# A hybrid decoder layer on one core: a third k pair by seven products in V, two in the attention's output, and another order of the sums

## The chip, the cores and the metric

The kernel runs on one core of a Trainium2 chip. The metric is the device time of one execution in microseconds (us), lower is better. Before the change three runs took 1879.17, 1879.82 and 1880.22 us; the median is 1879.82. One further execution was taken by the hardware profiler; all profile rows are of it. The engines in the rows are PE (TensorE, matmuls), PEld (its weight loads), DVE (VectorE), ACT (ScalarE), POOL (GpSimd) and SP (SyncE, which issues the DMAs here).

## The reference

One layer on a residual stream of 256 tokens x 2048 channels, in float32. Weights and activations are float32, and the output too.

```
h = rmsnorm(x, g_mix);  proj = h @ w_in                # 2048 -> 2816+2816+5*2048
x_r, g_r, q, k, v, gate_r, gate_a = split(proj)
y_r = gelu(g_r) * rg_lru(causal_conv(x_r), ...)        # recurrent mixer
y_r = y_r @ w_rnn_out                                  # 2816 -> 2048
o   = stick_breaking_attention(norm(q), norm(k), v)    # 16 heads of 128
y_a = o @ w_attn_out                                   # 2048 -> 2048
x   = x + (sigmoid(gate_r) * y_r + sigmoid(gate_a) * y_a) @ w_o
g, u = split(rmsnorm(x, g_ffn) @ w_ffn_gu)             # 2048 -> 2 * 5632
x   = x + (silu(g) * u) @ w_ffn_down
x   = x + sigmoid(rmsnorm(x, g_ple) @ w_ple_gate) * (p @ w_ple_proj)
```

## The kernel before

**Precision.** TensorE multiplies a reduced float32 (fp32r). Each float32 operand is held as two such halves, hi (a rounded copy) and lo (the rest). A product of two operands is three matmuls into one PSUM bank, hi x hi, hi x lo and lo x hi (`prod`, L576 to L578), each 128x128 by 128x512.

**Weights.** All weights lie in one array in the order of use, cut into chunks of 128x1024 (512 KB). `Stream` brings them in: SP issues each chunk's DMA into one of 4 raw buffers (tile name `w`), ACT makes the high half (`whi`, L307) and DVE the low half (`wlo`, L308), each with 4 buffers. Splits run 3 chunks ahead of the matmuls and DMAs 4 more ahead. SP issues all DMAs in one order, each after its buffer came free. Activations, and raw weight blocks that are needed for sums, live in a pool of 26 tiles of 128x1024 (`Q`) and one of 21 tiles of 128x512 (`H`).

**Groups.** Wide products (`group`) make 256 tokens x 1024 columns at a time: two column halves of 512 and two token halves of 128, so four PSUM banks (the kernel names them 2, 4, 3, 8). A group works through a list of slots. A plain slot is one k tile of 128 input channels: 1 chunk and 12 matmuls. A pair of k tiles together with the two token halves and the two column halves is a 2x2 by 2x2 block product, which can be made by seven products in place of eight: 21 matmuls in place of 24. It needs sums of the weight blocks (made by DVE on the raw blocks, then split like a chunk) and sums of the activations (`half_sums`, called through `parts_sums`: an add of hi and lo, four 128x128 ops, an ACT copy, a DVE subtract), and four results that are shared: the products "11", T1, T2 and T3 are copied out of PSUM by ACT, and `whole` adds them to the four banks with four DVE ops.

**The lists.** `SEVEN` has two pairs of k tiles and 12 plain ones. A string names a slot for both pairs: "11", "21" and "22" are raw blocks (128x1024, one half for each pair), T1 starts as the raw block "12"; the rest are sums made in place by DVE (L291): T1 = 12 + 11, then T2, T3 and T4. `SEVEN3` has a third pair, whose seven products come in the slots ("S", 1, 2) to ("S", 4, 2): S1 and S2 are two raw chunks; for S2 DVE makes Y, a new `Q` tile, with two 512-wide adds (L266), S3 is S2 summed in place by one add, and S4 a half of Y with one more add. `LONG` is the list with two pairs of the recurrent output (ro). `pairs_of` names the pairs that a stage makes by seven products.

**The stages,** in the order in which PE runs them: a first gate block (gtr), the recurrent branch, the recurrent output (ro0, ro1), V (v0, v1), the blocks of Q, K and the attention's gate with the attention of eight pairs of heads worked in between (`step`, by the table `at`), the attention's output (ao0, ao1), w_o (wo0, wo1), gate-up groups gu0 to gu3, down (dn0), gu4 to gu7, down (dn1), gu8 to gu10, down (dn2), and the last gate (pg). A group number stands behind the stage's name.

**Around V.** The activation sums of V's pairs are made during the second recurrent output group (`also`, two of its slots). After each V group `whole` gives four result blocks, and each of them becomes one `Q` tile: ACT writes a scaled high half and DVE (L384) the low half.

**Around the attention's output.** `ost` holds the attention's output as eight `Q` tiles of hi and lo. Before, the two groups use a plain list, and each bank is multiplied by its gate (`gta`) and added to the gated recurrent output. `next_mix`, put in `pend` and taken by the next group's slots from the fourth on, turns a pair of these results by PE (L1041) for w_o.

**Order.** Each engine runs its instructions in the order of its own program. Where DVE's and ACT's instructions stand among each other was fixed when the kernel was built, by a scheduler with a model of their times; a tile that is asked for later in the code takes its place in the pool later.

Of the kernel before, what the change touches and what calls it, by code (L numbers as in the profile page):

```python
# [11 lines left out]
ALU = mybir.AluOpType  # L12

P = 128
S = 256
# [9 lines left out]
KD = D // P  # L25
# [5 lines left out]
FQ0 = [0, 16, 32]  # L31
NG = 11
SEVEN = ["11", "T1", "21", 4, 5, "22", 6, 7, "T2", 8, 9, "T3", 10, 11, "T4", 12, 13, 14, 15]
SEVEN3 = ["11", ("S", 1, 2), "T1", "21", ("S", 2, 2), 6, "T2", 7, "22", 8, ("S", 3, 2), 9, "T3", 10,
          ("S", 4, 2), 11, "T4", 12, 13, 14, 15]
def ONE(k):

    return [("S", 1), ("S", 2), k + 2, k + 3, k + 4, ("S", 3), k + 5, k + 6, ("S", 4), *range(k + 7, k + 12)]


LONG = ["11", "T1", "21", 4, 5, "22", 6, 7, 8, "T2", 9, 10, 11, "T3", 12, 13, 14, "T4", 15, 16, 17, 18, 19, 20, 21]
# [6 lines left out]
def pairs_of(name):  # L48

    if name[:2] == "dn":  # L50
        q = int(name[2])
        return [FQ0[q] // 2 + i for i in range(2 if FQ[q] == 16 else 1)]
    return (0, 1, 2) if name == "gu" else (0, 1)


def is_sum(x):

    return isinstance(x, str) or isinstance(x, tuple) and x[0] == "S"
# [14 lines left out]
C_XR, C_GR, C_Q, C_K, C_V, C_GTR, C_GTA = 0, 22, 44, 60, 76, 92, 108  # L73
# [87 lines left out]
def tail():  # L161


    def wide(name, w, slots, c=0):
        return [(name, g, w, c + 8 * g, c + 8 * g + 4, slots[g]) for g in range(2)]

    def blocks(*cs):
        return [("blk", b, None, c, None, None) for c, b in cs]

    def gu(*gs):  # L170
        return [("gu", g, "gu", 4 * g, 44 + 4 * g, SEVEN3) for g in gs]

    def dn(q):
        k, p = FQ0[q], FQ0[q] // 2
        slots = [x if isinstance(x, str) else x + k for x in SEVEN] if FQ[q] == 16 else [
            x if isinstance(x, int) else x + (p,) for x in ONE(k)]
        return wide(f"dn{q}", "dn", [slots] * 2)

    x = [("x", 0), ("x", 1)]
    plain = [list(range(KD))] * 2  # L180
    return (wide("ro", "ro", [LONG] * 2) + wide("v", "in", [SEVEN] * 2, C_V)
            + blocks(*[(c, b) for b in range(4) for c in (C_Q, C_K)], *[(C_GTA, b) for b in range(4)])
            + wide("ao", "ao", plain) + wide("wo", "wo", [SEVEN] * 2) + gu(0, 1, 2, 3) + dn(0) + gu(4, 5, 6, 7) + dn(1)
            + gu(8, 9, 10) + dn(2)
            + wide("pg", "pg", [SEVEN[:-3] + x + SEVEN[-3:]] * 2))

# [167 lines left out]
def tile_hybrid_block(ctx: ExitStack, tc: tile.TileContext, xT: bass.AP, x: bass.AP, pT: bass.AP,  # L354
# [18 lines left out]
    def psum():  # L373
        cnt[0] += 1
        return pps.tile([P, 512], F32, tag="ps", name=f"ps_{cnt[0]}")
# [4 lines left out]
    def tt(o, a, b, op):  # L380
        nc.vector.tensor_tensor(o, a, b, op)  # L381
# [4 lines left out]
    def actv(o, i, f, **kw):  # L386
        nc.scalar.activation(o, i, f, **kw)  # L387
# [234 lines left out]
    xg = []  # L622
# [20 lines left out]
    def group(at, pairs, sums, after=None, also=()):  # L643

        name, g = at  # L650
        slots = [x for n, y, _, _, _, sl in HEAD + TAIL if (n, y) == at for x in sl
                 if isinstance(x, int) or is_sum(x)]
        seq = [(n, q) for n, x in enumerate(slots) for q in products(x, pairs_of(name)[:2])]
        if at == LAST_GROUP:
            k = len(slots) - 3
            rest = [q for q in seq if q[0] >= k]
            seq = [q for q in seq if q[0] < k] + [q for b in "2438" for q in rest if q[1][0] == b]
        first, last = {}, {}
        for i, (_, (b, y, _, _)) in enumerate(seq):
            first.setdefault(b, i)  # L660
            last[b] = i
            if y in ("11", "T1", "T2", "T3"):
                last[y] = i
        plain8 = [i for i, (_, (b, y, _, _)) in enumerate(seq) if b == "8" and not isinstance(y, str)]
        assert "11" not in last or last["T1"] < plain8[0]
        banks, tile_, got = {}, {}, {}
        for i, (n, (b, y, p, c)) in enumerate(seq):
            if n not in got:
                if n in also:
                    also[n]()  # L670
                if n >= 3 and pend:
                    pend.pop(0)()
                got[n] = S_.take(("tok", name, g, slots[n]))
            if b not in banks:
                banks[b] = psum()
            ps = banks[b]
            if p is None:
                o = tok(pairs, *y)
            else:
                o = {"11": tok(pairs, 2 * p, 0), "21": tok(pairs, 2 * p + 1, 0), "22": sums[p][3],  # L680
                     "T1": sums[p][0], "T2": sums[p][1], "T3": sums[p][2],
                     "T4": tok(pairs, 2 * p + 1, 1)}[y]
            _, _, hi, lo, w0 = got[n].columns(c)
            s = slice(w0, w0 + 512)
            prod(ps, o, hi[:, s], lo[:, s], i == first[b], i in (last[b], last.get(y)),
                 b in "B8")
            if y in ("11", "T1", "T2", "T3") and i == last[y]:
                t = tile_[y] = tl("T")
                actv(t, ps, AF.Copy)
                if y == "T2":  # L690
                    tt(tile_["T1"], tile_["T1"], t, ALU.subtract)
                if y == "T3" and after is not None:
                    after(tile_)
        return [banks[b] for b in "2438"], tile_


    xc, xcs, gel, y, gtr, ysum, xsum = {}, {}, {}, [], [], {}, {}
# [120 lines left out]
    also = {max(1, 2 * i - 4): [later(next_xg)] for i in range(2, NPD)}  # L818
    for i in range(NPD):
        also.setdefault(2 * i + 1 if i < 7 else 14, []).append(squares_x(i))  # L820
    also = {n: (lambda fs: lambda: [f() for f in fs])(fs) for n, fs in also.items()}
# [38 lines left out]
    def whole(at, pairs, sums, also=()):  # L860

        (q2, q4, q3, q8), t = group(at, pairs, sums, None, also)
        c11, c21, c12, c22 = t["11"], t["T2"], t["T1"], t["T3"]
        tt(c11, q2, c11, ALU.add)
        tt(c21, q4, c22, ALU.add)
        tt(c12, q3, c12, ALU.add)
        tt(c22, q8, c22, ALU.subtract)
        return c11, c21, c12, c22

    def parts_sums(pairs, sums, p):  # L870
        h = tl("T")
        hi, lo = parts(pairs[p])
        tt(pair(h), f32(hi), f32(lo), ALU.add)
        sums[p] = half_sums(h)
# [8 lines left out]

    n = len(LONG)
    for g in range(2):
        also = {n - 2 + i: (lambda p: lambda: parts_sums(xg, xsum, p))(p) for i, p in enumerate(pairs_of("v"))} if g else {
            8: last_gate, 12: next_table}
        for i, c in enumerate(whole(("ro", g), y, ysum, also)):
            o = gtr[2 * g + i // 2][i % 2]
            tt(o, c, o, ALU.mult)  # L890
# [3 lines left out]
    for g in range(2):  # L894
        for i, c in enumerate(whole(("v", g), xg, xsum)):
            r = rs_x(i % 2)
            v = tl("B", F32R)
# [5 lines left out]
    qs, ks, zst, ost = {}, {}, {}, []  # L903
# [111 lines left out]
    at = {}  # L1015
    for hp in range(NHP):
        for d, f in enumerate(ATT_AT):
            at.setdefault(18 + 9 * hp + f, []).append(((att_t, att_z, att_e, att_o)[d], hp))
    slot = [0]

    def step():
# [28 lines left out]
        return run  # L1050

    for g in range(2):
        for i, ps in enumerate(group(("ao", g), ost, None)[0]):
            c, m = gta[2 * g + i // 2][i % 2], mix_r[2 * g + i // 2][i % 2]
            tt(c, ps, c, ALU.mult)
            tt(c, c, m, ALU.add)
        pend.extend(next_mix(p) for p in range(4 * g, 4 * g + 4))

# [69 lines left out]
    def gu(g):  # L1128
        also = {}
        if g in behind:  # L1130
            also = {17 + i: (lambda p: lambda: parts_sums(acts, asum, p))(p)
                    for i, p in enumerate(pairs_of(f"dn{behind[g]}"))}
        c11, c21, c12, c22 = whole(("gu", g), hg, hsum, also)
        for c, t in ((c11, 0), (c21, 1)):
            actv(c, c, AF.Silu, scale=rs1[:, t:t + 1])
        for c, t, s_ in ((c12, 0, c11), (c22, 1, c21)):
            stt(c, c, rs1[:, t:t + 1], s_, ALU.mult, ALU.mult)

        def turn(f):
            def run():  # L1140
                ps = psum()
                for e in range(2):
                    for t, a in enumerate((c12, c22)):
                        c = (2 * f + e) * P
                        o = e * 256 + t * P
                        nc.tensor.transpose(ps[:, o:o + P], a[:, c:c + P], ident)  # L1146
                acts[2 * g + f] = split(ps, "A")
            return run

        pend.extend(turn(f) for f in range(2))  # L1150
# [41 lines left out]
    for g in range(2):  # L1192
        qs_, t_ = group(("pg", g), h3, sum3, also={len(SEVEN) - 3: embedded(g)})
        for n, (q, c, op) in enumerate(zip(qs_, ("11", "T3", "T1", "T3"), (ALU.add,) * 3 + (ALU.subtract,))):
            t, b = n % 2, 2 * g + n // 2
            c, ps, o = t_[c], pp.pop(0), tl("T")
# [70 lines left out]
```

## Time and profile before

| | |
|---|---|
| three runs | 1879.17, 1879.82, 1880.22 us, median 1879.82 |
| the profiled execution | 1879.71 us, of which the span is 1878.0 |
| granted clock of TensorE, mean | 0.999 |
| HBM traffic | 357.69 MB read, 192 GB/s over the span |
| w<-in_w_dram, chunks of 512 KB | 538, 4.1 us from issue to landing (median) |
| Q<-in_w_dram, raw blocks of 512 KB | 118, 6.2 us (median) |

How to read the rows: in the groups of instructions, "out<-in" gives the names of the tiles, then shape and count; then busy time in us and the mean of one in ns; then the idle time of the engine just before these instructions and what ended most of it. In a timeline, the columns are start and length in us, engine, line, operation, tiles, shape and count of neighbouring equal ones, and in brackets the idle time before with its releaser. A matmul's length in the rows (0.39) is longer than its spacing, since matmuls are pipelined. The windows give the busy time of each engine, with its count of instructions, in one stretch of the span.

Stages by the first matmul of each, in us of the span: gtr 5.53; ro0 390.54, ro1 449.02; v0 507.50, v1 549.66; Q, K and the gate from 591.82; ao0 890.14, ao1 933.66; wo0 979.12, wo1 1023.20; gu0 1067.24, gu1 1110.66; dn0 1237.90; gu4 1323.20; dn1 1492.78; gu8 1578.08; dn2 1705.76; pg 1772.49.

### The profile page before, as it was taken

Reading aid. Unit: us, or ns where it says so; the run is one execution under the profiler, and the core shown is the slowest. Engines: PE = TensorE matmul, PEld = TensorE weight load, DVE = VectorE, ACT = ScalarE, POOL = GpSimd, SP = SyncE. Lnnn points to the kernel's source line nnn. Section 1 sums busy time; section 2 is a strip of 40 time slices with the busy share of each in tenths; the row PEclk is TensorE's granted clock in tenths of the full one; section 3 lists DMA queues with packets and bytes.
Section 4 is the critical chain, followed back from the end, with each engine's and each line's share of the span. In section 5 each row is a group of like instructions: output and inputs, shape, how many; then the busy total and the mean of one; then the engine's idle time right before and its main releaser. Section 6 shows DMA issues by size and latency. Waiting matters only on the chain.

```text
span 1878.0 us, 24098 instructions
## 1 busy us (share of the span) xinstructions
PE 1866.8 (99%) x8970; PEld 1570.1 (84%) x8970; DVE 1440.0 (77%) x1741; ACT 1187.3 (63%) x1580; POOL 2.2 (0%) x9
## 2 busy tenths in 40 slices
PE   9999999999999999999999999999999999999998
PEld 7899989888888888888888888888888888888886
DVE  7688887677776576665578988887888978888876
ACT  6688888764555566676356765565556655565763
POOL 0000000000000000000000000000000000000000
PEclk9999999999999999999999999999999999999999
DMA  7556556666546555445566566466454566545554
GB/s 280 176 182 197 192 176 195 228 212 191 210 154 192 190 163 159 166 158 172 187 217 224 196 224 220 169 212 243 173 180 179 180 221 238 188 150 189 180 192 144
DMA packets 101925, 361.36 MB, mean 192 GB/s; under 512 B 11440, under 2 KB 12080, under 8 KB 101808
## 3 DMA queue, kind: packets, MB, share of 16 engines
q1 hardware_dynamic: 101664, 359.82, 56.2%
q8 instruction: 70, 1.15, 0.2%
q14 instruction: 47, 0.39, 0.1%
q10 hardware_dynamic: 144, 0.01, 0.0%
HBM read 357.69 MB, written 2.10 MB: 192 GB/s over the span
## 4 chain that ended last, share of the span: by engine, by line
PE 97%; DVE 1%; DMA 1%; issue 0%; SPq 0%; ACT 0%; DVEq 0%
PE ps L577 26%; PE ps L578 26%; PE ps L576 26%; PE ps L506 9%; PE ps L510 4%; PE ps L490 1%; PE ps L489 1%; PE ps L488 1%; DMA Q<-in_w_dram 1%; DVE wlo L308 1%; DVE H L381 1%; PE ps L1146 1%; PE ps L930 0%; PE ps L1088 0%; DMA w<-in_w_dram 0%; DVE Q L291 0%
## 5 line engine op out<-in xcount | busy, mean ns | idle before, releaser
L308 DVE TENSOR_TENSOR wlo<-w,whi 128x1024 fp32r<-128x1024 f32 (+2 forms) x560 | 675.8, 1214 | 289.7 <-ACT whi L307 284.7
L577 PE MATMUL ps<-wlo,Q 128*128 128x512 f32 x2213 | 863.2, 390 | 1.3 <-DVE wlo L308 1.1
L578 PE MATMUL ps<-whi,Q 128*128 128x512 f32 x2213 | 861.8, 390 | 0.0
L307 ACT ACTIVATE whi<-w 128x1024 fp32r<-128x1024 f32 (+2 forms) x560 | 586.0, 1052 | 371.2 <-PE ps L578 324.3
L576 PE MATMUL ps<-whi,Q 128*128 128x512 f32 x2213 | 765.5, 391 | 0.3 <-ACT whi L307 0.3
L577 PEld LDWEIGHTS ps<-wlo,Q 128*128 128x128 f32 x2213 | 415.6, 188 | 87.9 <-DVE wlo L308 3.3
L578 PEld LDWEIGHTS ps<-whi,Q 128*128 128x128 f32 x2213 | 415.5, 188 | 86.1
L576 PEld LDWEIGHTS ps<-whi,Q 128*128 128x128 f32 x2213 | 414.7, 188 | 85.7 <-ACT whi L307 1.0
L307 ACT ACTIVATE whi<-Q 128x1024 fp32r<-128x1024 f32 (+1 forms) x213 | 219.8, 1033 | 182.2 <-PE ps L578 140.3
L308 DVE TENSOR_TENSOR wlo<-Q,whi 128x1024 fp32r<-128x1024 f32 (+1 forms) x213 | 253.1, 1189 | 64.6 <-ACT whi L307 64.5
L506 PE MATMUL ps<-Q,whi 128*128 128x512 f32 x704 | 170.7, 392 | 0.0
L506 PEld LDWEIGHTS ps<-Q,whi 128*128 128x128 f32 x704 | 128.8, 188 | 24.5
L291 DVE TENSOR_TENSOR Q<-Q,Q 128x1024 f32<-128x1024 f32 x92 | 112.4, 1221 | 1.6 <-DMA Q<-in_w_dram 0.3
L387 ACT ACTIVATE H<-ps 128x512 f32<-128x512 f32 (+1 forms) x150 | 77.0, 531 | 57.6 <-PE ps L578 39.5
L381 DVE TENSOR_TENSOR H<-ps,H 128x512 f32<-128x512 f32 (+1 forms) x158 | 90.8, 603 | 19.2 <-PE ps L578 10.1
L510 PEld LDWEIGHTS ps<-Q,wlo 128*128 128x128 f32 x704 | 90.4, 191 | 3.5
L381 DVE TENSOR_TENSOR H<-H,H 128x512 f32<-128x512 f32 (+2 forms) x151 | 88.7, 597 | 5.8 <-ACT H L387 5.1
L510 PE MATMUL ps<-Q,wlo 128*128 128x256 f32 x704 | 91.5, 283 | 0.0
L387 ACT ACT_TABLE_LOAD x53 | 68.0, 1283 | 0.9
L387 ACT ACTIVATE Q<-H 128x512 fp32r<-128x512 f32 x46 | 28.2, 623 | 26.4 <-DVE H L381 25.8
L490 PE MATMUL ps<-Q,wlo 128*128 128x256 f32 x140 | 39.6, 283 | 0.0
L489 PE MATMUL ps<-Q,whi 128*128 128x256 f32 x140 | 39.6, 283 | 0.0
(132 smaller groups left out, 883.1 us busy)
## 6 DMA issues: line engine op xcount, KB each, us to landing
w<-in_w_dram SPq DMA_DIRECT2D x538, 512.0 KB, 4.1
Q<-in_w_dram SPq DMA_DIRECT2D x118, 512.0 KB, 6.2
w<-in_w_dram SPq DMA_DIRECT2D x16, 448.0 KB, 3.2
H<-in_x_dram SPq DMA_DIRECT2D x8, 256.0 KB, 5.8
H<-in_xT_dram SPq DMA_DIRECT2D x7, 256.0 KB, 6.8
out_dram<-H SPq DMA_DIRECT2D x7, 256.0 KB, 3.6
w<-in_w_dram SPq DMA_DIRECT2D x4, 320.0 KB, 4.2
w<-in_w_dram SPq DMA_DIRECT2D x2, 256.0 KB, 3.0
```

Of the source, the lines that this page charges most:

```text
L291: self.nc.vector.tensor_tensor(r[o], r[o], r[a], ALU.add)
L307: self.hi_ins = self.nc.scalar.activation(hi[:, :c], t[:, :c], AF.Copy)
L308: self.lo_ins = self.nc.vector.tensor_tensor(lo[:, :c], t[:, :c], hi[:, :c].bitcast(F32), ALU.subtract)
L381: nc.vector.tensor_tensor(o, a, b, op)
L387: nc.scalar.activation(o, i, f, **kw)
L489: nc.tensor.matmul(o, wt[0], xl, start=False, stop=False)
L490: nc.tensor.matmul(o, wt[1], xh, start=False, stop=stop)
L506: nc.tensor.matmul(pss[e], wt[0], rhs(xs, k), start=(k == 0), stop=(k == n - 1))
L510: nc.tensor.matmul(pss[e][:, :256], wt[1], rhs(xs, k)[:, :256], start=False, stop=False)
L576: nc.tensor.matmul(ps, x[0], wh, start=start, stop=False, skip_group_check=goes_on)
L577: nc.tensor.matmul(ps, x[0], wl, start=False, stop=False, skip_group_check=goes_on)
L578: nc.tensor.matmul(ps, x[1], wh, start=False, stop=stop, skip_group_check=goes_on)
```

## The change

- `pairs_of` gives V three pairs, and V's two groups use `SEVEN3` in place of `SEVEN`.
- `SEVEN3` itself has another order: the raw block "21" comes behind S2 and slot 6, where it stood ahead of both. This holds for V and for all 11 gate-up groups.
- The attention's output uses `SEVEN` in place of the plain list; its results come through `whole`, and its activation sums are made by two steps in the last block of the attention's gate.
- In the second recurrent output group the activation sums of V start one slot earlier, since there are three.

```diff
-SEVEN3 = ["11", ("S", 1, 2), "T1", "21", ("S", 2, 2), 6, "T2", 7, "22", 8, ("S", 3, 2), 9, "T3", 10,
+SEVEN3 = ["11", ("S", 1, 2), "T1", ("S", 2, 2), 6, "21", "T2", 7, "22", 8, ("S", 3, 2), 9, "T3", 10,
           ("S", 4, 2), 11, "T4", 12, 13, 14, 15]
...
-    return (0, 1, 2) if name == "gu" else (0, 1)
+    return (0, 1, 2) if name in ("gu", "v") else (0, 1)
...
-    plain = [list(range(KD))] * 2
-    return (wide("ro", "ro", [LONG] * 2) + wide("v", "in", [SEVEN] * 2, C_V)
+    return (wide("ro", "ro", [LONG] * 2) + wide("v", "in", [SEVEN3] * 2, C_V)
...
-            + wide("ao", "ao", plain) + wide("wo", "wo", [SEVEN] * 2) + gu(0, 1, 2, 3) + dn(0) + gu(4, 5, 6, 7) + dn(1)
+            + wide("ao", "ao", [SEVEN] * 2) + wide("wo", "wo", [SEVEN] * 2) + gu(0, 1, 2, 3) + dn(0) + gu(4, 5, 6, 7) + dn(1)
...
-        also = {n - 2 + i: (lambda p: lambda: parts_sums(xg, xsum, p))(p) for i, p in enumerate(pairs_of("v"))} if g else {
+        also = {n - 3 + i: (lambda p: lambda: parts_sums(xg, xsum, p))(p) for i, p in enumerate(pairs_of("v"))} if g else {
...
+    osum = {}
+    for i, p in enumerate(pairs_of("ao")):
+        at[93 + i] = [(lambda p: parts_sums(ost, osum, p), p)]
...
-        for i, ps in enumerate(group(("ao", g), ost, None)[0]):
+        for i, o in enumerate(whole(("ao", g), ost, osum)):
             c, m = gta[2 * g + i // 2][i % 2], mix_r[2 * g + i // 2][i % 2]
-            tt(c, ps, c, ALU.mult)
+            tt(c, o, c, ALU.mult)
             tt(c, c, m, ALU.add)
```

In the changed program PE has 18 matmuls fewer. DVE has 54 instructions more and ACT 21 more; the DMAs are as many as before, and 12 of the chunks go to a `Q` tile in place of a raw buffer.

## The prediction, made before the changed kernel was run

> **What bounds the kernel now.** I read the page's first rows and its chain of waits, then PE's groups by line, then the stages cut into windows, then PE's, DVE's and ACT's timelines where groups begin.
>
> ```profile
> span 1878.0 us, 24098 instructions
> PE 1866.8 (99%) x8970; PEld 1570.1 (84%) x8970; DVE 1440.0 (77%) x1741; ACT 1187.3 (63%) x1580; POOL 2.2 (0%) x9
> PE 97%; DVE 1%; DMA 1%; issue 0%; SPq 0%; ACT 0%; DVEq 0%
> L577 PE MATMUL ps<-wlo,Q 128*128 128x512 f32 x2213 | 863.2, 390 | 1.3 <-DVE wlo L308 1.1
> ```
>
> PE is busy 99% of the span and makes 97% of the chain that ended last; its wait for the weights' low halves (wlo) is 1.1 us in all. So PE's program sets the time. The windows of the two V groups, of the second group of the attention's output (ao1), and of the gate-up groups 4 and 8 (gu4, gu8) give the price of a matmul and show where PE isn't full:
>
> ```profile
> core 0: us, PE busy (x) PEld busy (x) DVE busy (x) ACT busy (x) POOL busy (x), PEclk, DMA share, GB/s
> 507.50:549.66 42.16, 42.16 (x188) 34.92 (x186) 32.83 (x33) 22.73 (x24) 0.00 (x0) 1.00 0.46 150
> 549.66:591.82 42.16, 42.16 (x188) 34.92 (x186) 30.67 (x31) 24.44 (x27) 0.00 (x0) 1.00 0.56 172
> 933.66:979.12 45.46, 45.46 (x209) 37.61 (x208) 31.93 (x41) 21.23 (x24) 0.00 (x0) 1.00 0.67 231
> 1323.20:1365.52 42.32, 41.82 (x184) 34.22 (x183) 34.51 (x35) 24.09 (x26) 0.00 (x0) 1.00 0.37 124
> 1578.08:1620.92 42.84, 42.11 (x184) 34.16 (x183) 35.00 (x36) 24.09 (x26) 0.00 (x0) 1.00 0.39 123
> ```
>
> A V group is 186 weight loads in 42.16 us: 0.2267 us a matmul with no gap (the 390 ns of the group's row overlap). Groups gu4 and gu8 have 183 weight loads, worth 41.49 us, and last 42.32 and 42.84: PE stands idle there 0.83 and 1.35 us. DVE is the next engine, with 33 of 42 us in V. Its order within a group's first 10 us decides whether the halves come in time.
>
> **The change part by part.** Removed: a k pair by seven products costs 21 matmuls instead of 24. V gets one more pair in 2 groups (2 x 3), the attention's output two pairs in 2 groups (2 x 6): 18 matmuls x 0.2267 = **-4.08 us**. Added: for each pair, DVE sums on raw weights (128x1024) and activations, and low halves; the weights loaded are the same. These cost nothing while DVE stays ahead of PE; the beginnings of groups are where it might not, so I set the changed program order of DVE against PE's there.
>
> *The second V group (v1).* The rows of DVE, then ACT, where v1 begins now (first matmul 549.66), and two of DVE's where gate-up group 1 (gu1) begins (first matmul 1110.66), which already has three pairs:
>
> ```profile
> 547.82 0.69 DVE L381 TENSOR_TENSOR H<-ps,H 128x512 f32<-128x512 f32 x1
> 548.42 1.22 DVE L291 TENSOR_TENSOR Q<-Q,Q 128x1024 f32<-128x1024 f32 x1
> 549.56 1.22 DVE L308 TENSOR_TENSOR wlo<-Q,whi 128x1024 fp32r<-128x1024 f32 x1
> 550.69 1.28 DVE L381 TENSOR_TENSOR H<-ps,H 128x512 f32<-128x512 f32 x2
> 551.89 0.74 DVE L384 SCALAR_TENSOR_TENSOR Q<-H,rstd_tok,Q 128x512 fp32r<-128x512 f32 x1
> 552.55 1.22 DVE L308 TENSOR_TENSOR wlo<-w,whi 128x1024 fp32r<-128x1024 f32 x1
> 549.90 1.06 ACT L307 ACTIVATE whi<-w 128x1024 fp32r<-128x1024 f32 x1 [0.64 <-PE ps L578]
> 551.22 0.60 ACT L387 ACTIVATE H<-ps 128x512 f32<-128x512 f32 x1 [0.25 <-PE ps L578]
> 1108.82 0.69 DVE L381 TENSOR_TENSOR H<-ps,H 128x512 f32<-128x512 f32 x1
> 1109.43 1.22 DVE L308 TENSOR_TENSOR wlo<-Q,whi 128x1024 fp32r<-128x1024 f32 x1
> ```
>
> From start to start a 1024-wide op takes 1.13 (549.56 to 550.69), a 512-wide one 0.60 (547.82 to 548.42), an output's low half (L384) 0.66 (551.89 to 552.55). With three pairs the low half of T1 starts 1.23 us before the group's first matmul (1109.43 against 1110.66), behind the add that waits for the last group's bank (1108.82). In v1's changed order twelve ops then stand ahead of the low half of S2, the third pair's second block: six 512-wide (three of the last group's result blocks, three on the raw sums Y and S3), the four outputs' low halves, and the adds of T2 and T3: 6 x 0.60 + 4 x 0.66 + 2 x 1.13 = 8.50 us. Counted from v1's first matmul: T1 done -1.23 + 1.13 = -0.10, S2's low half starts 8.40 and ends 9.62 (1.22 long). Those twelve are queued there because Y gets its tile only behind the four output tiles, and S2 is read from Y. PE's 24th matmul wants it at 23 x 0.2267 = 5.21: **+4.41 us**, PE idle in pieces. The first piece is S2's high half: ACT has four outputs and a copy of the bank of "11" ahead of it, and Y's second add ends about 5.6 by the same addition, so the half is ready 1.06 later, 6.65, and wanted at 18 x 0.2267 = 4.08: 2.6 us. Behind it nothing else is late: block 6's low half starts 1.13 later and is wanted five matmuls later, which is as long. With each row at its full length (0.69, 0.74, 1.22) the twelve take 9.5 and the stall is 5.5; below, zero, were Y ready before the outputs.
>
> *The first V group (v0).* Five 512-wide ops and one add stand between T1 and S2, one more 512-wide op ahead of block 6: S2 ends at -0.10 + 3.00 + 1.13 + 1.22 = 5.25 (due 5.21), block 6 at 6.98 (due at the 30th matmul, 6.57): **+0.41**, between 0 and 1.2.
>
> *The reordered gate-up groups.* The timelines of gu4 (first matmul 1323.20) and gu8, PE's rows at the stall, then DVE's:
>
> ```profile
> 1329.58 0.39 PE L576 MATMUL ps<-whi,Q 128*128 128x512 f32 x1
> 1330.47 0.50 PE L577 MATMUL ps<-wlo,Q 128*128 128x512 f32 x1 [0.50 <-DVE wlo L308]
> 1584.84 0.39 PE L576 MATMUL ps<-whi,Q 128*128 128x512 f32 x1
> 1585.84 0.50 PE L577 MATMUL ps<-wlo,Q 128*128 128x512 f32 x1 [0.62 <-DVE wlo L308]
> 1319.31 0.69 DVE L266 TENSOR_TENSOR Q<-Q,Q 128x512 f32<-128x512 f32 x1 [0.49 <-DMA Q<-in_w_dram]
> 1324.00 1.22 DVE L308 TENSOR_TENSOR wlo<-Q,whi 128x1024 fp32r<-128x1024 f32 x1
> 1325.13 1.88 DVE L381 TENSOR_TENSOR H<-ps,H 128x512 f32<-128x512 f32 x3
> 1326.92 1.22 DVE L308 TENSOR_TENSOR wlo<-Q,whi 128x1024 fp32r<-128x1024 f32 x1
> 1574.69 0.69 DVE L266 TENSOR_TENSOR Q<-Q,Q 128x512 f32<-128x512 f32 x1 [0.99 <-DMA Q<-in_w_dram]
> ```
>
> Here DVE is late because a sum for the next group waited 0.49 and 0.99 us for its raw block. The new order puts S2 in the place of "21" (1326.92, done 4.94, due 5.21), and block 6 two 1024-wide ops behind it: 3.72 + 2 x 1.13 + 1.22 = 7.20, due 6.34: 0.86 us late if DVE is as late as now. But the raw block that it waits for now leaves SP's queue one transfer earlier, and then 0.49 and 0.99 go. If all goes, gu4 is 0.4 late and gu8 0.5 in place of 0.83 and 1.35, -1.3; if none, about +0.2. I take **-0.9**; the bounds are -2.2 (no stall left) and +0.2. In the eight steady groups the moved "21" is wanted 16 matmuls (3.6 us) later, which is more than the two 1024-wide ops it is put behind: nothing. With gu0: 0.1.
>
> *The first output group (wo0),* behind the last "ao" group, whose four results now need an add each:
>
> ```profile
> 979.02 1.22 DVE L308 TENSOR_TENSOR wlo<-Q,whi 128x1024 fp32r<-128x1024 f32 x1
> 980.16 0.68 DVE L381 TENSOR_TENSOR H<-ps,H 128x512 f32<-128x512 f32 x1
> 981.36 1.28 DVE L381 TENSOR_TENSOR H<-ps,H 128x512 f32<-128x512 f32 x2
> ```
>
> Behind the low half of "21" (979.02, 0.10 before the group) there are now seven 512-wide ops and the low half of block 4 ahead of the last mixed gate, which PE's transposes want at the 27th matmul: 1.03 + 7 x 0.60 + 1.13 + 0.08 = 6.44 against 5.89: **+0.55**, between 0 and 1.2. The sums for the pairs of "ao" fall in the last gate block, whose DVE has slack, so I cost them at nothing; without it two of them would be some 2.2 us each, three 512-wide ops and four small ones.
>
> Sum: -4.08 + 4.41 + 0.41 - 0.9 + 0.1 + 0.55 = +0.49. The profiled execution took 1879.71 us (span 1878.0 and 1.71 around it), 0.11 under the median 1879.82: **1880.2 us**.
>
> This takes starts to starts. The Trainium skill, "VectorE: DVE Perf Modes", section "The DRAIN you can't avoid", has it that the next op doesn't start until the pipe is empty; in these rows the next starts about 0.09 us before the row's end. By that rule the sum would be that of the second rival, by the rows it is the one above.
>
> **The rivals.** *V's stalls don't come*: 1879.71 - 4.08 - 0.9 + 0.1 + 0.55 = 1875.4. For it: the windows show V's groups without one idle instant, and DVE 9 us free in each. Against it: the slack is in the later slots, and the engine takes its ops in program order.
>
> *Every DVE op in front of a late half costs its whole row*, since sums are read soon after they are written (Y, T2, "whole" blocks): then slower. v1 +1.07, v0 +0.75, block 6 in gu4 and gu8 +0.5 each, wo0 +0.66, together 3.5: 1883.7. It decides from the point where an op needs the one just ahead of it; against it, the rows above overlap by 0.09 everywhere.
>
> *The clock falls in v1's idle time.* The start of the span shows what a cold TensorE does:
>
> ```profile
> 1.55 4.18 PE L618 MATMUL ps<-w1h,ones_r 128*128 128x512 f32 x9 [1.55 <-DVE ones_r L428]
> 5.53 1.31 PE L576 MATMUL ps<-whi,Q 128*128 128x512 f32 x4
> ```
>
> Nine matmuls take 4.18 us there, 0.46 each. Four microseconds at that pace hold 8.6 matmuls, worth 1.95 at 0.2267: 2.05 lost, 1882.2. Against it: gu8's 1.35 idle left its clock at 1.00. The Trainium skill, "TensorE: Matmul & The Clock Gate", section "HAM oscillation — how this bites in real kernels", warns of idle gaps over some 3.4 us; my longest piece is 2.6, so by that rule the price is nil, though the pieces together pass it; no run here shows such a gap.
>
> **How the numbers follow.** My forecast 0.46, with a range of its own from 1877.9 to 1882.7 (the gate-up groups, v0 and wo0 all at their lower or all at their upper bounds); no stall in V 0.17; whole rows 0.24; the clock 0.07; anything later still, as a raw block that misses v1's adds, 0.06. Of 0.2%, 3.76 us, about what a measurement of this kernel can tell from no change: under 1876.06 is faster, over 1883.58 slower. Faster: 0.16 of the first rival and 0.01 of the forecast, 0.17. Slower: 0.15 of the whole rows, 0.02 of the clock, the last 0.06: 0.23. The same: 0.60. The range from 1875.2 to 1884.0 holds the first rival's time and the second's.
>
> **What would show it.** In v1, PE waits for S2's high half some 2.6 us, then for low halves, and its window lasts 42.16 - 0.68 + 4.4 = 45.9; without that wait I am wrong by most of the sum. v0's window is about 41.9. gu4 and gu8 no longer wait at S2 but at block 6, with the waits of 0.49 and 0.99 us for the raw block gone or shorter. wo0's transposes wait for an add. Both "ao" groups lose 1.36 us (ao1's 45.46 becomes 44.10). The granted clock stays 1.00 in v1; if it falls, the third rival. DVE's starts behind T1 in v1 at 0.60 and 1.13 speak for the forecast, at 0.69 and 1.22 for the second.

## The result and the profile after

The changed kernel takes 1884.64 us (median of 12 runs, 1883.68 to 1885.80) against 1879.78 before (12 runs, 1879.17 to 1881.22): 1.0024 times as long, 95% interval 1.0015 to 1.0033. It is slower, by somewhat more than the 0.2% that the prediction named as the bound, and 0.64 us outside the predicted range. Its profiled execution took 1884.45 us. The page of the changed kernel begins so (the lines of its code have moved by one: hi x hi is L575, hi x lo L576, lo x hi L577, the low halves are L307):

```profile
span 1882.7 us, 24154 instructions
PE 1868.3 (99%) x8952; PEld 1568.4 (83%) x8952; DVE 1474.3 (78%) x1795; ACT 1203.4 (64%) x1601; POOL 2.7 (0%) x9
L576 PE MATMUL ps<-wlo,Q 128*128 128x512 f32 x2207 | 863.4, 391 | 1.1 <-DVE wlo L307 1.1
L575 PE MATMUL ps<-whi,Q 128*128 128x512 f32 x2207 | 753.3, 392 | 3.3 <-ACT whi L306 2.8
```

PE has 18 instructions less and is busy 1.5 us *longer*, in a span that is 4.7 us longer. Its waits for low halves are the same 1.1 us; the wait for high halves has grown from 0.3 to 2.8 us. Waits alone are not 4.7 us plus the 4.1 that the missing matmuls were worth, so part of the loss must look like work. Where it lies is seen best from the distance between the first matmuls of two stages, taken from the trace for every stage. Differences to the kernel before, in us; stages not named differ by 0.05 or less:

| stage | of it, matmuls removed | difference | left |
|---|---|---|---|
| gtr (start) | 0 | -0.35 | -0.35 |
| v0 | -0.68 | -0.08 | +0.60 |
| v1 | -0.68 | +6.16 | **+6.84** |
| ao0, ao1 | -2.72 | -1.36, -1.27 | +0.09 |
| wo0 | 0 | +0.77 | +0.77 |
| gu0 | 0 | +0.29 | +0.29 |
| gu4, gu8 | 0 | +0.91, -0.37 | +0.54 |

Almost all of it is v1. The start (gtr) is no effect of the change: in the profiled executions of the other kernels below it differs by -0.21 to +0.57. The changed kernel's windows: v1 as a whole, then stretches of it.

```profile
core 0: us, PE busy (x) PEld busy (x) DVE busy (x) ACT busy (x) POOL busy (x), PEclk, DMA share, GB/s
549.22:597.54 48.32, 45.25 (x185) 36.08 (x183) 36.13 (x38) 26.24 (x29) 0.00 (x0) 0.93 0.37 129
553.00:556.00 3.00, 0.46 (x3) 0.04 (x1) 3.00 (x5) 1.05 (x2) 0.00 (x0) 1.00 0.00 0
556.00:557.00 1.00, 0.73 (x2) 0.30 (x2) 1.00 (x2) 1.00 (x3) 0.00 (x0) 0.94 0.00 0
557.00:558.00 1.00, 0.99 (x2) 0.83 (x3) 1.00 (x2) 1.00 (x2) 0.00 (x0) 0.50 0.00 0
563.00:564.00 1.00, 1.00 (x5) 0.78 (x4) 1.00 (x2) 0.00 (x0) 0.00 (x0) 0.65 0.04 16
564.00:565.00 1.00, 1.00 (x6) 0.83 (x5) 1.00 (x2) 0.13 (x1) 0.00 (x0) 1.00 0.00 0
```

Two things are to be seen. From 553 to 556 PE has three matmuls while DVE is busy without a gap: PE waits for DVE's queue. And behind it the granted clock is 0.50 from about 557 until 563.7. PE counts as busy in those microseconds, which is why the busy time rose: a matmul at half the clock is "work" in the page. PE's timeline in the changed v1 (first matmul 549.22):

```profile
553.07 0.39 PE L577 MATMUL ps<-whi,Q 128*128 128x512 f32 x1
556.05 0.73 PE L575 MATMUL ps<-whi,Q 128*128 128x512 f32 x2 [2.59 <-ACT whi L306]
557.00 1.65 PE L575 MATMUL ps<-whi,Q 128*128 128x512 f32 x3 [0.22 <-ACT whi L306]
558.91 0.79 PE L576 MATMUL ps<-wlo,Q 128*128 128x512 f32 x1 [0.26 <-DVE wlo L307]
560.36 0.63 PE L577 MATMUL ps<-whi,Q 128*128 128x512 f32 x1
560.78 0.63 PE L575 MATMUL ps<-whi,Q 128*128 128x512 f32 x1
```

S2's high half is awaited for 2.59 us; the first matmul with S2's low half comes at 558.91, which is 9.69 us into the group, where 5.21 was due: 4.48 us of wait. From there the pitch is 0.43 us (560.36 to 560.78), not 0.2267. From the 36th matmul on the pace is whole again; until then that costs another 2.36: 4.48 + 2.36 = 6.84. DVE's timeline, and ACT's row of S2's high half, in the same stretch:

```profile
547.99 1.22 DVE L307 TENSOR_TENSOR wlo<-Q,whi 128x1024 fp32r<-128x1024 f32 x1
549.12 1.28 DVE L380 TENSOR_TENSOR H<-ps,H 128x512 f32<-128x512 f32 x2
551.58 1.41 DVE L383 SCALAR_TENSOR_TENSOR Q<-H,rstd_tok,Q 128x512 fp32r<-128x512 f32 x2
554.16 0.69 DVE L265 TENSOR_TENSOR Q<-Q,Q 128x512 f32<-128x512 f32 x1
555.37 2.36 DVE L290 TENSOR_TENSOR Q<-Q,Q 128x1024 f32<-128x1024 f32 x2
557.64 1.22 DVE L307 TENSOR_TENSOR wlo<-Q,whi 128x1024 fp32r<-128x1024 f32 x1
554.95 1.06 ACT L306 ACTIVATE whi<-Q 128x1024 fp32r<-128x1024 f32 x1 [2.28 <-DVE Q L265]
```

T1's low half starts at 547.99 (1.23 before the group, as forecast), twelve ops follow without a gap, and S2's low half starts at 557.64, 8.42 into the group, where 8.40 was forecast. Y's second add is the row at 554.16; ACT has waited 2.28 us for it when it makes S2's high half at 554.95.

In gu4 (first matmul 1327.40), DVE and one row of PE:

```profile
1323.08 0.69 DVE L265 TENSOR_TENSOR Q<-Q,Q 128x512 f32<-128x512 f32 x1 [1.31 <-DMA Q<-in_w_dram]
1323.68 1.22 DVE L290 TENSOR_TENSOR Q<-Q,Q 128x1024 f32<-128x1024 f32 x1
1328.89 1.22 DVE L307 TENSOR_TENSOR wlo<-Q,whi 128x1024 fp32r<-128x1024 f32 x1
1334.09 1.22 DVE L307 TENSOR_TENSOR wlo<-w,whi 128x1024 fp32r<-128x1024 f32 x1
1335.37 0.50 PE L576 MATMUL ps<-wlo,Q 128*128 128x512 f32 x1 [0.35 <-DVE wlo L307]
```

The sum that waits for a raw block is still there, and DVE now waits 1.31 us for it where it waited 0.49. This wait ends 4.32 us ahead of the group, against 3.89 before, so the block is there earlier by 0.4 us. But the sum now stands *ahead* of an add for this group (1323.68), which was in front of it before. T1's low half starts 1.49 us into the group, and it was 0.80. In wo0 the transposes wait for an add, as was forecast:

```profile
988.82 0.30 PE L1043 MATMUL ps<-ident,H 128*128 128x128 f32 x1 [0.55 <-DVE H L380]
```

### The profile page after: what moved, and what is told of

The parts are those of the page before. It is cut to its first block, busy times and chain, and to the rows that moved or that the text cites. A ratio compares the mean times of both kernels' runs of the same rounds, so it can differ in the third digit from the quotient of the medians.

```text
span 1882.7 us, 24154 instructions
## 1 busy us (share of the span) xinstructions
PE 1868.3 (99%) x8952; PEld 1568.4 (83%) x8952; DVE 1474.3 (78%) x1795; ACT 1203.4 (64%) x1601; POOL 2.7 (0%) x9
## 4 chain that ended last, share of the span: by engine, by line
PE 96%; DVE 2%; DMA 1%; issue 0%; ACT 0%; DVEq 0%; SPq 0%
PE ps L576 26%; PE ps L577 26%; PE ps L575 26%; PE ps L505 9%; PE ps L509 4%; PE ps L489 1%; PE ps L488 1%; PE ps L487 1%; DMA Q<-in_w_dram 1%; DVE H L380 1%; DVE wlo L307 1%; PE ps L1148 1%; PE ps L1090 0%; PE ps L929 0%; DVE Q L290 0%
## 5 line engine op out<-in xcount | busy, mean ns | idle before, releaser
L576 PE MATMUL ps<-wlo,Q 128*128 128x512 f32 x2207 | 863.4, 391 | 1.1 <-DVE wlo L307 1.1
L307 DVE TENSOR_TENSOR wlo<-w,whi 128x1024 fp32r<-128x1024 f32 (+2 forms) x548 | 661.4, 1214 | 253.8 <-ACT whi L306 248.7
L577 PE MATMUL ps<-whi,Q 128*128 128x512 f32 x2207 | 860.1, 390 | 0.0
L306 ACT ACTIVATE whi<-w 128x1024 fp32r<-128x1024 f32 (+2 forms) x548 | 573.1, 1051 | 330.5 <-PE ps L577 289.8
L575 PE MATMUL ps<-whi,Q 128*128 128x512 f32 x2207 | 753.3, 392 | 3.3 <-ACT whi L306 2.8
L575 PEld LDWEIGHTS ps<-whi,Q 128*128 128x128 f32 x2207 | 414.0, 188 | 91.0 <-ACT whi L306 4.5
L576 PEld LDWEIGHTS ps<-wlo,Q 128*128 128x128 f32 x2207 | 415.2, 188 | 88.5 <-DVE wlo L307 3.5
L577 PEld LDWEIGHTS ps<-whi,Q 128*128 128x128 f32 x2207 | 415.1, 188 | 85.4
L306 ACT ACTIVATE whi<-Q 128x1024 fp32r<-128x1024 f32 (+1 forms) x235 | 242.0, 1032 | 209.2 <-PE ps L577 168.3
L307 DVE TENSOR_TENSOR wlo<-Q,whi 128x1024 fp32r<-128x1024 f32 (+1 forms) x235 | 278.9, 1188 | 70.6 <-ACT whi L306 70.5
L290 DVE TENSOR_TENSOR Q<-Q,Q 128x1024 f32<-128x1024 f32 x100 | 122.1, 1222 | 1.6 <-DMA Q<-in_w_dram 0.3
L386 ACT ACTIVATE H<-ps 128x512 f32<-128x512 f32 (+1 forms) x158 | 81.9, 535 | 56.9 <-PE ps L577 37.9
L380 DVE TENSOR_TENSOR H<-H,H 128x512 f32<-128x512 f32 (+2 forms) x167 | 96.9, 592 | 6.0 <-ACT H L386 5.5
```

Of the source, the lines that this page charges most:

```text
L290: self.nc.vector.tensor_tensor(r[o], r[o], r[a], ALU.add)
L306: self.hi_ins = self.nc.scalar.activation(hi[:, :c], t[:, :c], AF.Copy)
L307: self.lo_ins = self.nc.vector.tensor_tensor(lo[:, :c], t[:, :c], hi[:, :c].bitcast(F32), ALU.subtract)
L575: nc.tensor.matmul(ps, x[0], wh, start=start, stop=False, skip_group_check=goes_on)
L576: nc.tensor.matmul(ps, x[0], wl, start=False, stop=False, skip_group_check=goes_on)
L577: nc.tensor.matmul(ps, x[1], wh, start=False, stop=stop, skip_group_check=goes_on)
```

## The experiments

All times are medians; each run stands beside runs of the kernel before on the same chip, and the ratio is to those. Eleven and five idle matmuls, the order alone and the attention's output alone ran beside a median of 1880.01; seventeen idle matmuls, V in the old order and the two kernels with late outputs beside 1879.98.

**Is the slow pace in v1 due to the idle time?** Idle matmuls were put ahead of S2's first product, where PE waits, `N` of them in a bank that the first real product overwrites. The rest of the change is as it is.

```diff
+                if at == ("v", 1) and slots[n] == ("S", 2, 2):
+                    banks["4"] = psum()
+                    for _ in range(N):
+                        nc.tensor.matmul(banks["4"], ones_r, w1t[0], start=True, stop=True)
```

Eleven:

> The changed kernel with eleven idle matmuls put into v1 ahead of S2's first product (into a bank that the first real product overwrites). Theory: v1's 6.2 us more are a wait of 4.5 us on the sums queued ahead of S2, and 2.35 us of a halved clock that the wait of 2.6 us in one piece sets off. The eleven (2.5 us) stand where PE waited anyway, so the wait's end doesn't move, the granted clock stays 1.00, and v1's window goes from 48.3 to 46.0 us: 1882.3 in all. Rival: the matmuls from S2 on are slow for another reason (their operands, the transfers at that time); then the clock or the pace is as before and the time stays at 1884.6, or rises.

Five:

> The same with five idle matmuls (1.1 us), so that the longest idle piece in v1 is about 1.6 us in place of 2.6, and the pieces behind it are as before. If the clock falls by the longest piece and 1.6 is short enough, it stays at 1.00: 1882.3. If it falls by the idle time summed over some microseconds (still 3 us here), it falls again: 1884.6, v1's window 48.3.

Eleven, and six more on block 6's high half, so that no long piece is left:

```diff
+                if at == ("v", 1) and slots[n] == 6:
+                    _, _, h6, _, _ = got[n].columns(0)
+                    banks["3"] = psum()
+                    for _ in range(6):
+                        nc.tensor.matmul(banks["3"], ones_r, h6[:, :512], start=True, stop=True)
```

> The changed kernel with eleven idle matmuls ahead of S2's first product and six more between block 6's high half and its third product, so that PE has no idle piece over 0.5 us in v1 while the waits end when they did. Theory: the clock stays 1.00 in every run, v1's window is 46.0 us (4.5 of waits, no slow matmul), the time 1882.3. Rival (the slow matmuls come with the place, not with the idle time): the clock falls, 1884.6.

Windows of v1 with eleven, a piece of it, then v1 with five and with seventeen idle matmuls:

```profile
549.43:597.14 47.71, 46.44 (x195) 37.32 (x194) 36.14 (x38) 26.25 (x29) 0.00 (x0) 0.96 0.42 131
560.00:561.00 1.00, 1.00 (x4) 0.79 (x3) 1.00 (x2) 0.60 (x1) 0.00 (x0) 0.50 0.00 0
549.81:595.92 46.11, 43.49 (x190) 35.01 (x188) 35.78 (x38) 26.14 (x29) 0.00 (x0) 1.00 0.43 136
549.67:595.91 46.24, 45.92 (x202) 37.38 (x200) 35.77 (x38) 26.16 (x29) 0.00 (x0) 1.00 0.43 135
```

With seventeen the granted clock stays at 1.00 in v1, and v1 is 2.1 us shorter although seventeen more matmuls run in it. The last of the six end 0.27 us after the low half was there, so the price of the clock is about the 2.36 read above. The mean clock of the ten runs is 0.999 in every one; in the twelve runs of the change it was 0.997 in eleven and 0.998 in one. (0.998 alone tells nothing: the late-output kernel below has it without a fall in v1, because the clock also falls behind the last matmul.) The time is 1883.18 (1.0015 times the kernel before, 1.0005 to 1.0024), 0.9 us over the expectation; in the profiled execution gu8 lost 0.7 more than in the change. The rival, that the place makes matmuls slow, is out.

The other two tell against the simple rule that the longest idle piece decides. With five, PE's waits in v1 are 1.46, 0.22 and 0.94 us, and in the profiled execution the clock held. With eleven, they are 0.21 and 0.94, and it fell from about 559.3 to 562.7. The ten runs with five spread from 1881.28 to 1885.98 at mean clocks of 0.997 to 0.999 (median 1884.03; in the profiled one dn1 is 1.27 us longer, behind a wait of 1.98 for a raw block), so from one execution to the next it may fall or not; with eleven, 1881.69 to 1883.81 (1882.97). My expectation of 1882.3 for eleven and of one or the other for five was too plain.

The traces hold the answer. In each of them the clock changes only on a grid of 3.413 us: in the changed kernel it is 1.00 for 549.546 us from its first record (161 steps), 0.50 for 6.827 (two) and 1.00 for 1314.131 (385); with eleven idle matmuls the fall lasts 3.413 (one). Where the grid lies differs from one execution to the next. Here are single steps of it, four of the changed kernel, two with eleven, two with five idle matmuls:

```profile
553.47:556.88 3.41, 0.73 (x2) 0.30 (x2) 3.41 (x6) 1.94 (x3) 0.00 (x0) 1.00 0.00 0
556.88:560.30 3.42, 3.03 (x6) 1.99 (x7) 3.42 (x4) 2.10 (x4) 0.00 (x0) 0.50 0.00 0
560.30:563.71 3.41, 3.41 (x9) 2.63 (x8) 3.41 (x4) 1.52 (x2) 0.00 (x0) 0.50 0.42 154
563.71:567.12 3.41, 3.41 (x16) 2.81 (x15) 2.59 (x4) 2.12 (x2) 0.00 (x0) 1.00 0.39 154
555.89:559.30 3.41, 2.14 (x8) 0.96 (x7) 3.41 (x4) 3.17 (x4) 0.00 (x0) 1.00 0.00 0
559.30:562.71 3.41, 3.41 (x9) 2.65 (x10) 3.41 (x4) 1.65 (x2) 0.00 (x0) 0.50 0.34 94
553.59:557.00 3.41, 1.95 (x10) 1.27 (x8) 3.41 (x5) 1.46 (x2) 0.00 (x0) 1.00 0.00 0
557.00:560.41 3.41, 2.25 (x9) 1.25 (x8) 3.41 (x4) 2.56 (x4) 0.00 (x0) 1.00 0.00 0
```

PE's x also counts matmuls that began before the step. Those that begin in it are 2, 6, 8 and 15 in the changed kernel, 6 and 8 with eleven, 8 and 7 with five. In all 14 traces every step in which six or fewer matmuls began was followed by 0.50, and every one with seven or more by 1.00; a step at 0.50 that is full holds eight, so the clock then returns. PE's idle time in a step, by the rows, doesn't separate them (1.27 us with eleven and it fell, 1.46 with five and it held). So, as far as these traces go, what counts is how many matmuls begin in a step, and where the steps lie decides the rest. In the change only five matmuls begin between 553.30 and 558.91, and wherever a grid of 3.413 is laid over PE's timeline, one step has at most five: it must fall. With seventeen the poorest step has at least eleven: it can't. With five idle matmuls six or fewer come in 0.75 of the grid's places, with eleven in 0.30 (the fallen stretch put back to the whole pace); the mean clock was 0.999 in four and in seven of their ten runs. The rule was read from the traces afterwards; no run was made to test it.

**Which part costs what?** SEVEN3's order alone, and the attention's output alone, on the kernel before (the first hunk of the change, and its hunks on `ao`, `osum` and the loop over the groups of "ao"):

> The kernel before with only SEVEN3's new order, so the eleven gate-up groups. Theory: the new order helps no steady group, and where DVE is late (gu4, gu8) it puts block 6 behind one more sum and an add in front that waits for a raw block: together +0.5 us as in the changed kernel, 1880.3. Rival, as predicted: the raw block comes earlier and both groups gain, -0.9: 1878.9.

> The kernel before with only the attention's output by two pairs of seven products. Theory: 12 matmuls less, 2.72 us, and given back 0.77 at wo0 (transposes that wait for the last gate's add): 1877.9, ao0 and ao1 1.3 to 1.4 us shorter each. Rival: with V as before, DVE's queue ahead of wo0 is the same, but the loss of 0.3 at gu0 comes from here too: 1878.2; or nothing is given back, 1877.1.

The order alone: 1880.83 us, 1.0007 (0.9998 to 1.0016), not to be told from no change. In its profile gu0 is +0.29, gu4 +0.67, gu8 -0.22; all others are within 0.11 of the kernel before. So it gained nothing, and gu0's loss comes from it. The attention's output alone: 1878.94 us, 0.9995 (0.9985 to 1.0004). Its windows are what was forecast, ao0 -1.36, ao1 -1.29, wo0 +0.77. The time is 1 us over the expectation and not to be told from no change either. In that profile gu4 is +0.85 with the old order. DVE's row ahead of gu4 there, and in the kernel further below whose gate-up groups have the old order and whose gu4 is +1.93:

```profile
1318.64 0.69 DVE L265 TENSOR_TENSOR Q<-Q,Q 128x512 f32<-128x512 f32 x1 [1.33 <-DMA Q<-in_w_dram]
1319.76 0.69 DVE L267 TENSOR_TENSOR Q<-Q,Q 128x512 f32<-128x512 f32 x1 [2.40 <-DMA Q<-in_w_dram]
```

In the kernel before this wait was 0.49: gu4 lost what the wait grew by. In the seven profiles with the new order in the gate-up groups and without the holding back that follows, gu4 is +0.66 to +0.99 and gu8 -0.83 to +0.33, so gu8 varies by 1.2 us with the order the same. Why the block comes later was not found.

**What makes v1's wait?** V's third pair in the old order, "21" ahead of S2, by a list of its own for V:

```diff
+SEVEN3V = ["11", ("S", 1, 2), "T1", "21", ("S", 2, 2), 6, "T2", 7, "22", 8, ("S", 3, 2), 9, "T3", 10,
+          ("S", 4, 2), 11, "T4", 12, 13, 14, 15]
-    return (wide("ro", "ro", [LONG] * 2) + wide("v", "in", [SEVEN3] * 2, C_V)
+    return (wide("ro", "ro", [LONG] * 2) + wide("v", "in", [SEVEN3V] * 2, C_V)
```

> The changed kernel with V's third pair in the old order of the sums ("21" ahead of S2), the gate-up groups in the new one. Theory: the twelve ops stand ahead of S2 in either order. One low half more is ahead of it, and it is due six matmuls later, so it ends at 10.75 where 6.57 is wanted: 4.2 us in place of 4.5, and the longest idle piece is shorter by what "21" fills, about 1.4 us; 1884.3 with the fall of the clock, 1882.0 without. Rival: the reordering made V's wait; then v1's window is about 42 and the time 1878.

1885.33 us, 1.0032 (1.0019 to 1.0045). PE's timeline where it waits, and v1's window:

```profile
560.14 2.59 PE L577 MATMUL ps<-whi,Q 128*128 128x512 f32 x5 [4.64 <-ACT whi L308]
549.90:599.16 49.26, 44.62 (x185) 36.12 (x183) 36.12 (x38) 26.01 (x29) 0.00 (x0) 0.93 0.41 127
```

The reordering did not make the wait; without it the wait is as bad. It is one piece now, not shorter as I expected, because here the two big adds stand even in front of Y's second add. Then the outputs were moved behind S2:

```diff
-            v = tl("B", F32R)
-            actv(v[:, :512], c, AF.Identity, scale=r)
-            stt(v[:, 512:], c, r, f32(v[:, :512]), ALU.mult, ALU.subtract)
-            vs.append(v)
+            def v_out(c=c, r=rs_x(i % 2)):
+                v = tl("B", F32R)
+                actv(v[:, :512], c, AF.Identity, scale=r)
+                stt(v[:, 512:], c, r, f32(v[:, :512]), ALU.mult, ALU.subtract)
+                vs.append(v)
+            if g == 0:
+                pend.append(v_out)
+            else:
+                v_out()
```

> The changed kernel, except that v0's four output tiles are made one by one in the slots of v1 from S2 on, so that Y gets its tile, and S2 its sum, ahead of them. Theory: S2's low half is then queued behind four 512-wide ops, one add and T1 only and ends 4.7 us after v1's first matmul (due 5.2), block 6 ends at 6.5 (due 6.3): v1 loses 0.2 us where it lost 6.8, the clock stays 1.00, and the time is 1884.6 - 6.7 = 1877.9. Rival: the outputs' work comes back as a wait at a later slot of v1, since DVE has the same work; then v1's window stays over 44 us and the time over 1880.

```profile
550.11:592.16 42.05, 41.79 (x185) 34.27 (x183) 32.73 (x34) 25.80 (x29) 0.00 (x0) 1.00 0.47 150
```

v1's window is 42.05 us where it was 48.32, the clock 1.00: the wait and the fall of the clock are gone but for 0.57 us over what 183 matmuls take (41.48), and the same DVE work is done behind it. The time is 1878.98, 0.9994 (0.9984 to 1.0004), not to be told from the kernel before, and 1 us more than expected: v0 lost 0.75 more, v1 0.4. Y of v1 now had its tile so early that its sums were put in front of v0. With the old order in the gate-up groups besides (`SEVEN3` as before, `SEVEN3V` with the new order for V):

> The same, and the gate-up groups keep the order they had; V alone has the new one. Theory: the new order gave the gate-up groups nothing, and cost about 0.5 us, so 1877.4, 2.4 us under the kernel before (18 matmuls, 4.1 us, less 0.8 at wo0, 0.6 in v0 and 0.2 in v1). Rival: gu4 and gu8 vary with the arrival of a raw block whatever the order; then as the run before, 1877.9.

1879.13 us, 0.9994 (0.9985 to 1.0004), no better; gu4 was +1.93 in its profile. The order is not what decides gu4; the wait for the raw block is, as shown above.

**Sums that stand too far ahead.** In v0, gu4 and gu8 the same thing is seen: a sum that is not due soon stands ahead of low halves that are. So sums were held back until a given low half is made, Y twelve chunks ahead of its slot and the others two to five. `los` lists the low halves as they are made, and `issue_after` keeps a sum behind one of them in the order that is fixed when the kernel is built (the lines that fill the list are left out):

```diff
+        back = {2: 12, 3: 5, "T2": 2, "T3": 4, "T4": 4}.get(x)
+        if back is None:
+            return self.sums_of(mode)
+        with self.tc.issue_after(self.los[self.n_split - back]):
+            return self.sums_of(mode)
```

It was tried with the late outputs, in the change as it is, and in the kernel before (medians of the kernel before beside them: 1880.13):

> The kernel of late_out, and DVE's sums on raw weights are held back: Y until the low half twelve chunks ahead of S2 is made, S3 five, T3 and T4 four, T2 two. Theory: what is left of the change's stalls comes from sums that stand too far ahead in DVE's order (next group's Y in front of gu4, gu8 and v0, T2's and T3's adds between T1 and S2), so v0 loses 1.3, wo0 0.5, gu4 and gu8 2.0 to 2.5 less, and v1 keeps 0 to 0.2: 1879.0 - 4.5 = 1874.5, faster than both kernels. Rival: held back, the sums come late for their own slots, and PE waits at T2 or S3; then the steady gate-up groups' windows grow over 42.4 us and the time is 1877 or more.

> The changed kernel with the same holding back, but v0's outputs where the change has them. Theory: of the twelve ops ahead of S2 in v1 the adds of T2 and T3 and of S3 go (2.9 us), so S2's low half would end at 6.8 in place of 9.6; but its high half still waits for Y, which waits for the outputs, so PE still idles 2.6 us at S2, then for block 6's high half, and v1 loses about 3.2 of waits in place of 4.5. If the clock falls by one idle piece of 2.6, 2 us more. With v0, wo0, gu4 and gu8 repaired (3.3 us): 1884.6 - 3.3 - 1.3 = 1880.0, or 1878 where the clock stays. Rival: the outputs weren't the cause, only the adds; then 1876.

> The kernel before with the same holding back. Theory: the waits of 0.8 us in gu4 and 1.3 us in gu8 belong to Y's place in DVE's order and not to SEVEN3's order, so both go: 1879.8 - 2.1 = 1877.7, gu4's and gu8's windows 41.5 us; wo0 loses its small wait, the rest is as before. Rival: the raw block itself is late; then PE waits at S2 in gu5 and gu9 and the time stays at 1879.8.

With late outputs: 1876.06 us, 0.9979 (0.9970 to 0.9988). In the change: 1879.71, 0.9998 (0.9989 to 1.0007); v1 still loses 5.01 us there by the table's last column, 3.56 of them up to S2's low half, and in the profiled execution its clock falls. So the outputs ahead of Y make most of the wait without those adds. In the kernel before: 1876.98, 0.9982 (0.9973 to 0.9992), gu4 -0.84 and gu8 -1.36. So gu4's and gu8's waits belong to the kernel before, and the raw block is not late for its own group. The first was 1.6 us over its expectation: wo0 got two waits of 0.4 and 0.7, and v1 kept 0.87 where at most 0.2 was expected. Left out for the attention's output and w_o:

```diff
-        if back is None:
+        if back is None or PLAN[CHUNKS[self.n_split][0]][0][1] in ("ao", "wo"):
```

> The kernel of pinned, but the sums of the attention's output and of w_o aren't held back. There the holding back put the last ao1 slot's matmuls into wo0 and left two waits of 0.4 and 0.7 us on low halves. Theory: with the old order of DVE there, ao1 and wo0 together go from 0.3 us over the kernel before to 0.5 under it, as in the changed kernel: 1876.1 - 0.8 = 1875.3. Rival: the waits come with the late outputs of V or with SEVEN in ao, not with the holding back; then 1876.1.

ao1 and wo0 are back at -1.27 and +0.78. 1875.56 us (1875.14 to 1875.87) beside 1880.03, 0.9974 (0.9963 to 0.9985), faster than both kernels. Its windows of v1, gu4 and gu8:

```profile
549.51:591.90 42.39, 42.15 (x185) 34.16 (x183) 34.29 (x36) 25.92 (x29) 0.00 (x0) 1.00 0.47 148
1321.33:1362.81 41.48, 41.48 (x185) 34.35 (x183) 34.24 (x35) 24.20 (x26) 0.00 (x0) 1.00 0.42 140
1575.31:1616.79 41.48, 41.48 (x185) 34.36 (x183) 34.24 (x35) 24.20 (x26) 0.00 (x0) 1.00 0.42 139
```

gu4 and gu8 are now what 183 matmuls take, 41.48 us. Of the 4.5 us under the kernel before, 3.1 are the holding back, which the kernel before can have too (1876.98 beside 1880.13); the change's own part, repaired, is about 1.3 of its 4.1 (1.7 between the two profiled executions). The two kernels did not run side by side, and the intervals of their ratios overlap.

## Why the prediction was wrong

The forecast was 0.5 us slower; the traces show 4.7 (first matmul to last). By its steps:

- *18 matmuls, -4.08*: right, as seen in the ao windows (-1.36, -1.27); in V the waits hide it, though v0 and v1 have three matmuls fewer each.
- *v1's wait, +4.41*: right, 4.48, in its place, size and parts (2.6 us at S2's high half). The cause, four outputs ahead of Y, was shown by moving them.
- *The clock*: this is the step that failed. It was the third rival, with a price of 2.05 and a chance of 0.07; it came, for 2.36, and the mean clock was 0.997 in eleven of the twelve runs, below every run of the kernel before that gives one (0.998 or 0.999). The pace in its price was sound, since it came from the start's own rows; that the sum came out near was partly luck: the fall lasted 6.83 us, not four, but the first 2.03 of them (556.88 to 558.91) lay in the wait for S2's low half. The chance wasn't sound: I held against it that gu8's 1.35 us had left the clock at 1.00, but that is half of the first piece alone that I had just forecast for v1, and in that kernel the poorest step of the grid around gu8 still has nine matmuls. The Trainium skill, "TensorE: Matmul & The Clock Gate", section "HAM oscillation — how this bites in real kernels", has gaps over some 3.4 us for the danger. Here the clock fell after a wait of 2.59 us, and in one execution with no wait over 0.94. The same page, section "What's actually happening", says that activity is counted in a window that runs freely; the traces agree, with steps of 3.413 us that lie elsewhere in each execution. But a step needn't be idle: the clock fell behind one in which six matmuls began.
- *gu4 and gu8, -0.9*: wrong in sign, +0.54 (+0.91 and -0.37). The raw block comes earlier in both, but the sum that waits for it was put ahead of another add in DVE's order, and in gu4 what PE gained by the block (0.4) it lost by the queue (an add of 1.13). By the spread of these two groups between the profiles above, the size of this step is not settled. I had counted the wait's length as given and set its place in the order aside, though the order was there to be read.
- *v0, +0.41, and wo0, +0.55*: 0.60 and 0.77, near. *gu0*: 0.29 where 0.1 was put for it and all others.
- *The second rival, whole rows for each op*: the range's upper end hung on it. DVE's starts in v1 are 0.60 and 1.13 apart, so it is out. The Trainium skill, "VectorE: DVE Perf Modes", section "The DRAIN you can't avoid", has the next op start when the pipe is empty, and adds that one that is not held starts earlier, which the prediction left out. The trace agrees with the addition: T1's low half starts at 547.99 and is 1.22 long, and the next op starts at 549.12, 1.13 later.

So the step that failed is the clock's: it was forecast to stay at 1.00, and it fell for two steps of 3.413 us. With the clock at its measured price and the rest as forecast the sum would have been 1882.6, inside the range; the 1.4 us of gu4 and gu8 take it to 1884.0, the range's end, and v0, wo0 and gu0 beyond.

## What to carry to other kernels

Where one engine sets the time, a stall's length is only part of its price: ask what the clock does after it. Count the matmuls that begin in any 3.4 us around the stall; if they can be six or fewer in a kernel like this one, take the stall away or fill it with idle matmuls. Shortening it is not enough: with five idle matmuls the grid's place decided. An added sum costs little where its engine has slack, but its place in that engine's queue counts, and so does the tile that it must wait for; read the order of the changed program around each group's first ten microseconds. A sum that is made long before it is due isn't free either: if its data are late, everything behind it is.

## What the hardware showed unexpectedly

After PE's wait of 2.59 us (and 0.22 and 0.26 behind it) the granted clock was 0.50 for 6.83 us, from 556.88 to 563.71; with idle matmuls in most of that wait it was still 0.50 for 3.41 us in one execution; with all of it filled it stayed at 1.00 in the profiled execution, and the mean clock was 0.999 in all ten. In the kernel with one wait of 4.64 us it fell during the wait. The falls begin and end on a grid of 3.413 us, and six matmuls in a step, where fifteen fit, did not keep the clock up, while seven did. The microseconds at half clock count as PE's busy time, so the page's share of PE, 99% before and after, shows nothing of it.
